# Small products of the triangular inverse, issued round the tiles of the array instead of tile by tile

## The chip, the cores and the metric

One core of a Trainium2 chip runs the whole model in one launch. The metric is the device time of an execution in microseconds; the figure for a kernel is the median of its runs.

## What is computed

Two layers of a diffusion block over 512 latent and 256 context tokens of width 1024. Each layer projects its normalised input once, runs three mixers in parallel on parts of the projection (neighbourhood attention, a bidirectional gated DeltaNet with four heads, a Fourier mixer), merges them by gates, and ends in an MLP. The change lies in the DeltaNet, whose recurrence is solved chunk by chunk:

```python
def _gated_delta_chunked(q, k, v, g, beta, s0):
    '''S_t = a_t (I - b_t k_t k_t^T) S_{t-1} + b_t k_t v_t^T, o_t = S_t^T q_t (chunked WY form)'''
    ...
    a_mat = jnp.where(strict, jnp.einsum('bhncd,bhnsd->bhncs', kb, k) * decay, 0.0) + jnp.eye(c, dtype=jnp.float32)
    rhs = jnp.concatenate([v * beta[..., None], kb * jnp.exp(g)[..., None]], axis=-1)
    sol = lax.linalg.triangular_solve(a_mat, rhs, left_side=True, lower=True)
    ...
    s_fin, o = lax.scan(step, s0, xs)
```

For each chunk a triangular matrix with ones on its diagonal must be solved against. The kernel inverts it instead and lets the scan multiply by the inverse.

## The kernel before

The kernel works in chunks of 128 tokens: six chunks and two directions make twelve blocks of 128x128 a head (`NU` is 12). `layer(l)` runs once a layer; in it, `by_clock` merges four generators by the times that they claim: `stream_dn` (the scan), `stream_prep` (what the scan needs, one `dn_prep(h)` for each of the four heads), `stream_na` (attention) and `stream_in` (input projections). This gives each instruction a priority, and a scheduler then orders the instructions of every engine by priority and by when their inputs can be ready. So the order on an engine isn't written out anywhere, and DMAs issued by SP form one queue of their own, in which a DMA that waits for its buffer holds back all behind it. A projection product (line 245, `ps_in`, `ps_inc`) is fed by `wload` (line 230): a weight load `wr` on SP, then a split into two parts on ScalarE and on VectorE or GpSimd.

`dn_prep(h)` does this: it loads the decay rows of its head twice, `Df` and `Db` (lines 531 and 532, SP); VectorE makes three decay masks of them (lines 538 to 540, `Dl` in a third buffer); products `ps_kk` give the triangular matrices `N` and the score matrices `PT`. The four 32x32 blocks on each diagonal go through DRAM (`nd`) to a layout with one block on a partition, VectorE inverts them, and they come back through `wd` into `N` and, transposed, into `Tst` (lines 592 and 593, eight DMAs on SP). Then the inverse is put together in two steps, the lines that the change touches:

- *32 to 64.* `ps_r` (line 601): for each of two quadrants `q`, twelve 32x32 products, at array position (32, 0) for the first and (96, 64) for the second; ScalarE copies each quadrant to `R` (603). `ps_w`: for each quadrant the products of line 609 at (0, 32) or (64, 96) and those of 613 at (0, 0) or (64, 64); 12 and 6 products for the first quadrant, 6 and 12 for the second; behind each quadrant ScalarE writes the results, negated, to `N` (616) and `Tst` (617).
- *64 to 128.* `ps_r2` (625): two groups of six 64x64 products at (64, 0), copied to `R` (627). `ps_w2` (630) at (0, 0) and `ps_w3` (636) at (0, 64), six products each, each in a PSUM tile of its own, copied out at 632 and 638. `L` is then copied from `Tst` (641, ScalarE) and `N` (642, VectorE); `dn_step` begins with products on it (`ps_ch`).

An array position (row, column) names the part of TensorE's 128x128 array that a product lies on: the row is that of its input partitions, the column that of its output partitions in PSUM. All PSUM tiles named here come from one tag with a single buffer (`pp`), so each waits for the one before to be read. `Df`, `Db`, `Dl`, the two blocks of the diagonal inverse and `R` share a tag of three SBUF buffers (`pr`), so the next head's loads wait for buffers of this head's inverse. All products here are float32.

Of the kernel before, what the change touches and what calls it, by code (L numbers as in the profile page):

```python
# [17 lines left out]
P = 128  # L18
# [19 lines left out]
# gates computed beside the mixers  # L38
NPRE = 16
# columns of the vector block  # L40
# [4 lines left out]
def kernel(ctx: ExitStack, tc: tile.TileContext, A: dict, out: bass.AP):  # L45
# [75 lines left out]
    def sigmoid_into(dst, src):  # L121
        """exp(min(x, 0) - log(1 + exp(-|x|))); dst is not src"""
        act.activation(out=dst, in_=src, func=AF.Abs)
        act.activation(out=dst, in_=dst, func=AF.Exp, scale=-1.0)
        act.activation(out=dst, in_=dst, func=AF.Ln, bias=1.0)
        dve.scalar_tensor_tensor(dst, in0=src, scalar=0.0, in1=dst, op0=ALU.min, op1=ALU.subtract)
        act.activation(out=dst, in_=dst, func=AF.Exp)

# [9 lines left out]
    def ada_block(l, q):  # L138
        """columns 512*q .. 512*q+511 of the adaLN projection of layer l, the contraction in four column groups"""
# [16 lines left out]
    def ada_group(l, q, lag):  # L156
        """four such blocks from the one at q, one in each column group; loads run lag rows of tiles ahead"""
# [26 lines left out]
    def ada_scale(l, i, k0=0, n=KD):  # L184
        """norm weight * (1 + scale) of the norm i of layer l"""
        sc = MOD[l][:, (3 * i + 1) * 8 + k0:(3 * i + 1) * 8 + k0 + n, :]
        g = vecs[l][:, (V_N1, V_N2)[i] + k0:(V_N1, V_N2)[i] + k0 + n]
        o = SC[l][i][:, k0:k0 + n, :]
        dve.tensor_scalar(o, sc, 1.0, None, op0=ALU.add)
        dve.tensor_tensor(o, o, g.unsqueeze(2).to_broadcast([P, n, 2]), op=ALU.mult)  # L190
# [22 lines left out]
    def ada_upto(l, q):  # L213
        """what follows needs the block q of layer l"""
# [8 lines left out]
    wcnt = [0]  # L223

    def wload(src, kn=KD):
        """[P, kn, 128] float32 -> for each k two float32r parts whose sum is the float32 one"""
# [13 lines left out]
    def proj(ps, w, kn, xh, xl, segs, off=0, k0=0, k1=KD):  # L240
        """ps[:, seg - off] = sum_k w[:, k].T @ x[k][:, seg], of it the part from k0 to k1"""
# [6 lines left out]
    def split_act(src, w, name, alloc):  # L248
        """float32 SBUF tile -> (hi, lo) tiles"""
# [7 lines left out]
    class Rms:  # L257
        """1 / rms of each token; the last of the tiles goes straight to the sum over partitions"""
# [33 lines left out]
    def mod_norm(l, i, xs, w, nm):  # L292
        """the modulated norm as two parts"""
# [24 lines left out]
    def modulate(k, x):  # L318
        """the first modulation, of a normalised tile that is no longer needed"""
# [10 lines left out]
    def by_clock(pri, *streams):  # L330
        """merge generators that yield the time of what they have emitted, by their clocks"""
# [33 lines left out]
    def layer(l):  # L365
# [39 lines left out]
        def gates():  # L405
# [40 lines left out]
            # rows of the summed log-decays, for a broadcast over partitions  # L446
# [7 lines left out]
        odn = drp.tile([NDH, P, TT], F32, tag="odn", bufs=1, name="odn")  # L454

        def conv_silu(ps, cw, w):
            """short conv over tokens and silu; the result at [0:512] and [514:770]"""
# [41 lines left out]
        def tok_major(src, offs, name, tag):  # L499
            """[feature, token] -> [token, 6, feature]"""  # L500
# [23 lines left out]
        def dn_prep(h, st):  # L524
# [41 lines left out]
            # inverses of the 32x32 diagonal blocks, one block on each partition  # L566
# [28 lines left out]
            # merge 32 -> 64  # L595
            R = U("R", tag="pr", w=NU * 64).rearrange("p (u c) -> p u c", c=64)
            ps = ps_aux("ps_r", "pp")
            for q in range(2):
                a, b = slice(64 * q, 64 * q + 32), slice(64 * q + 32, 64 * q + 64)
                for u in range(NU):  # L600
                    pe.matmul(ps[a, u * 32:u * 32 + 32], lhsT=Nu[b, u, a], rhs=Tst[b, u, b], start=True, stop=True,
                              tile_position=(64 * q + 32, 64 * q))
                act.copy(R[a, :, 0:32], ps[a, 0:NU * 32].rearrange("p (u c) -> p u c", c=32))
            ps = ps_aux("ps_w", "pp")
            for q in range(2):
                a, b = slice(64 * q, 64 * q + 32), slice(64 * q + 32, 64 * q + 64)
                ul = slice(0, NU) if q == 0 else slice(6, NU)
                for u in range(ul.start, ul.stop):
                    pe.matmul(ps[b, u * 32:u * 32 + 32], lhsT=R[a, u, 0:32], rhs=Nu[a, u, a], start=True, stop=True,
                              tile_position=(64 * q, 64 * q + 32))  # L610
                ut = slice(0, 6) if q == 0 else slice(0, NU)
                for u in range(ut.start, ut.stop):
                    pe.matmul(ps[a, u * 32:u * 32 + 32], lhsT=Nu[a, u, a], rhs=R[a, u, 0:32], start=True, stop=True,
                              tile_position=(64 * q, 64 * q))
                pv = ps[:, 0:NU * 32].rearrange("p (u c) -> p u c", c=32)
# [3 lines left out]
            # merge 64 -> 128  # L619
# [9 lines left out]
            for u in range(6):  # L629
                pe.matmul(ps[a, u * 64:u * 64 + 64], lhsT=Nu[a, u, a], rhs=R[a, u, :], start=True, stop=True,  # L630
                          tile_position=(0, 0))
            act.activation(out=Tst[a, 0:6, b], in_=ps[a, 0:384].rearrange("p (u c) -> p u c", c=64), func=AF.Copy,
                           scale=-1.0)
            ps = ps_aux("ps_w3", "pp")
            for u in range(6):
                pe.matmul(ps[b, u * 64:u * 64 + 64], lhsT=R[a, 6 + u, :], rhs=Nu[a, 6 + u, a], start=True, stop=True,
                          tile_position=(0, 64))
# [8 lines left out]
        def dn_step(h, st, d, step):  # L646
            """one chunk of the scan of direction d"""
# [95 lines left out]
        ona = drp.tile([4, P, TT], F32, tag="ona", bufs=1, name="ona")  # L743

        def na_in(c, st):
            # scores as products of two parts each: the two halves of a stack hold the parts of one head
# [37 lines left out]
        def na_pair(scores, n_loc, biases, vts, dst, view):  # L784
            """softmax over the keys of 128 queries for both heads of a pair; the outputs to dst, feature-major"""
# [85 lines left out]
        ofn = drp.tile([4, P, TT], F32, tag="ofn", bufs=1, name="ofn")  # L871

        def fourier():
# [34 lines left out]
            for i, (s0, n, tab) in enumerate(sets):  # L908
# [24 lines left out]
                for g in range(4):  # L933
# [9 lines left out]
                    else:  # L943
                        # the transform at (n - t, -f) is the one at (t, f); -f lies 64 rows away, but for 0 and 64
# [167 lines left out]
        for hb in range(4):  # L1112
# [12 lines left out]
            for k in range(KD):  # L1125
# [3 lines left out]
                # the last one in halves of the tokens, so that the final norm starts early  # L1129
# [43 lines left out]
    # the first products with the first half of the features, while the rest of the modulation comes  # L1173
# [28 lines left out]
def _prepare(inp):  # L1202
# [31 lines left out]
    # relative bias of the two kinds of query tiles; outside the window a constant  # L1234
# [60 lines left out]
```

## Time and profile before

| | us |
|---|---|
| median of three runs | 2771.27 (2769.14 to 2774.12) |
| span of the profiled execution, first to last instruction | 2750.2 |
| TensorE busy in it | 2618.0 |
| VectorE busy | 1391.2 |
| ScalarE busy | 1191.1 |
| GpSimd busy | 609.1 |

The profile comes from one execution. It gives the span of that execution and no device time beside it, so the difference to the median, 21.1 us, stands for what lies before the first and behind the last instruction. An engine's busy time is the time in which at least one of its instructions ran. The chain that ended last is followed back from the last instruction, at each step to what released it; work on it is work that the end waited for. In the timeline, records of one kind that follow each other are put together, with their number behind an x; a record of TensorE lasts longer than the distance to the next, since products overlap in its pipeline.

### The profile page before, as it was taken

What the parts mean: (1) busy time and instruction counts of PE and PEld (TensorE: products, weight loads), DVE (VectorE), ACT (ScalarE), POOL (GpSimd) and SP (SyncE); (2) the same over time, 40 slices, a digit from 0 to 9 for tenths busy, and PEclk for the clock granted to TensorE, in tenths of its full rate; (3) what the DMA queues carried; (4) which work ended last, traced back from release to release, by engine and by line L of the source; (5) the groups of instructions that cost most, each with busy time, mean ns of one, the idle gap of its engine ahead of it and who ended that gap; (6) DMA issues with size and microseconds to landing.
All of it is one profiled execution on the core that took longest, in us unless ns stands there. A gap on an engine that the chain in (4) does not pass through costs nothing.

```text
span 2750.2 us, 40072 instructions
## 1 busy us (share of the span) xinstructions
PE 2618.0 (95%) x15066; PEld 2103.9 (77%) x15066; DVE 1391.2 (51%) x2831; ACT 1191.1 (43%) x2430; POOL 609.1 (22%) x522
## 2 busy tenths in 40 slices
PE   6999999999999999999999988998999999999998
PEld 3877768677878777888888867776777777788886
DVE  5657576857423634222222365768677436433334
ACT  4546555555543224121222255455565654423333
POOL 3222212231111112111111123221323222222222
PEclk9999999999999999999999999999999999999999
DMA  6232222221255743342312223232232335333332
GB/s 219 81 87 68 78 58 75 71 71 53 68 197 189 255 139 115 104 135 91 120 59 66 81 60 111 72 81 58 79 85 63 93 112 187 96 95 96 96 96 88
DMA packets 196705, 278.41 MB, mean 101 GB/s; under 512 B 56768, under 2 KB 75936, under 8 KB 196512
## 3 DMA queue, kind: packets, MB, share of 16 engines
q1 hardware_dynamic: 196512, 275.87, 32.9%
q8 instruction: 118, 1.93, 0.3%
q14 instruction: 75, 0.61, 0.1%
HBM read 244.29 MB, written 27.31 MB: 99 GB/s over the span
## 4 chain that ended last, share of the span: by engine, by line
PE 73%; DVE 8%; ACT 3%; DMA 1%; issue 1%; POOL 1%; SPq 0%; DVEq 0%; ACTq 0%; POOLq 0%
PE ps_m L245 32%; PE ps_in L245 14%; PE ps_br L245 6%; PE ps_wo L245 4%; PE ps_inc L245 3%; PE ps_ada L168 1%; DVE cy L468 1%; PE ps_s L830 1%; PE ps_s L818 1%; PE ps_s L829 1%; PE ps_s L812 1%; DVE xn L303 1%; PE ps_ch L676 1%; DVE stmp L581 1%; DMA Db<-gdr 1%
## 5 line engine op out<-in xcount | busy, mean ns | idle before, releaser
L236 POOL TENSOR_TENSOR wlo<-wr,whi 128x512 fp32r<-128x512 f32 x360 | 484.8, 1348 | 1894.7 <-ACT whi L233 1789.7
L233 ACT CAST whi<-wr 128x512 fp32r<-128x512 f32 x560 | 346.3, 619 | 879.9 <-PE ps_m L245 519.8
L245 PE MATMUL ps_in<-hh,whi 128*128 128x512 f32 x960 | 381.0, 408 | 11.8 <-ACT kraw L750 5.5
L245 PE MATMUL ps_in<-hh,wlo 128*128 128x512 f32 x960 | 378.2, 404 | 2.2 <-POOL wlo L236 2.2
L245 PE MATMUL ps_in<-hl,whi 128*128 128x512 f32 x960 | 377.7, 404 | 0.0
L236 DVE TENSOR_TENSOR wlo<-wr,whi 128x512 fp32r<-128x512 f32 x200 | 138.6, 693 | 244.7 <-ACT whi L233 243.9
L245 PE MATMUL ps_m<-ml,whi 128*128 128x512 f32 (+1 forms) x768 | 233.8, 358 | 4.1 <-POOL ml L313 3.2
L245 PE MATMUL ps_m<-mh,whi 128*128 128x512 f32 (+1 forms) x768 | 233.0, 358 | 2.9 <-ACT mh L309 2.9
L245 PE MATMUL ps_m<-ah,wlo 128*128 128x512 f32 (+1 forms) x776 | 234.4, 355 | 0.0
L245 PE MATMUL ps_m<-ah,whi 128*128 128x512 f32 (+1 forms) x776 | 234.2, 355 | 0.0
L245 PE MATMUL ps_m<-al,whi 128*128 128x512 f32 (+1 forms) x776 | 233.2, 353 | 0.0
L245 PE MATMUL ps_m<-mh,wlo 128*128 128x512 f32 (+1 forms) x768 | 231.7, 355 | 0.0
L245 PEld LDWEIGHTS ps_in<-hh,whi 128*128 128x128 f32 x960 | 181.8, 194 | 48.1 <-ACT kraw L750 5.9
L245 PEld LDWEIGHTS ps_in<-hh,wlo 128*128 128x128 f32 x960 | 181.2, 193 | 36.5 <-POOL wlo L236 3.4
L245 PEld LDWEIGHTS ps_in<-hl,whi 128*128 128x128 f32 x960 | 181.4, 194 | 32.8 <-issue 2.0
L1134 DVE SCALAR_TENSOR_TENSOR x<-ps_m,mod,x 128x512 f32<-128x512 f32 (+1 forms) x97 | 60.8, 655 | 247.8 <-PE ps_m L245 247.8
L245 PEld LDWEIGHTS ps_m<-mh,whi 128*128 128x128 f32 x768 | 126.6, 189 | 35.3 <-ACT whi L233 8.4
L245 PEld LDWEIGHTS ps_m<-ah,whi 128*128 128x128 f32 x776 | 127.7, 188 | 28.9 <-ACT whi L233 6.7
L245 PE MATMUL ps_inc<-hh,whi 128*128 128x256 f32 x512 | 149.6, 292 | 0.0
L245 PEld LDWEIGHTS ps_m<-ml,whi 128*128 128x128 f32 x768 | 126.8, 188 | 29.5 <-POOL ml L313 6.0
L245 PE MATMUL ps_inc<-hl,whi 128*128 128x256 f32 x512 | 148.7, 290 | 0.0
L245 PE MATMUL ps_inc<-hh,wlo 128*128 128x256 f32 x512 | 147.0, 287 | 0.0
(325 smaller groups left out, 4927.3 us busy)
## 6 DMA issues: line engine op xcount, KB each, us to landing
wr<-in_w_dram SPq DMA_DIRECT2D x256, 256.0 KB
wr<-in_wi_dram SPq DMA_DIRECT2D x224, 256.0 KB
wada<-in_wa_dram SPq DMA_DIRECT2D x192, 256.0 KB
wr<-in_wb_dram SPq DMA_DIRECT2D x48, 256.0 KB
wr<-in_wo_dram SPq DMA_DIRECT2D x32, 256.0 KB
gpre<-sgp SPq DMA_DIRECT2D x16, 384.0 KB
sgg<-gpre SPq DMA_DIRECT2D x16, 384.0 KB
rot<-kn SPq DMA_DIRECT2D x64, 64.0 KB
```

What stands on the lines that cost most here:

```text
L168: pe.matmul(ps[32 * j:32 * j + 32, :], lhsT=cs[:, k, :], rhs=ws[k][j], start=(k == 0), stop=(k == KD - 1), tile_position=(0, 32 * j))
L233: act.copy(hi, raw)
L236: eng.tensor_tensor(lo, raw, hi.bitcast(F32), op=ALU.subtract)
L245: pe.matmul(ps[:, s0 - off:s1 - off], lhsT=a, rhs=b[k][:, s0:s1], start=(k == 0 and i == 0), stop=(k == kn - 1 and i == 2))
L303: dve.scalar_tensor_tensor(t[:, s0:s1], in0=xs[k][:, s0:s1], scalar=sc, in1=rs[:, s0:s1], op0=ALU.mult, op1=ALU.mult)
L468: dve.scalar_tensor_tensor(y[:, :n], in0=cin[:, j:j + n], scalar=vec[:, cw + j:cw + j + 1], in1=y[:, :n], op0=ALU.mult, op1=ALU.add)
L581: dve.tensor_tensor(tv, Nb[:, j + 1:32, j:j + 1].to_broadcast([48, n, m]), Wb[:, j:j + 1, 0:m].to_broadcast([48, n, m]), op=ALU.mult)
L676: pe.matmul(ps[:, 2 * P:3 * P], lhsT=kt, rhs=Uc, start=True, stop=True)
L812: pe.transpose(ps[:, i * P:(i + 1) * P], Pm[:, i * P:(i + 1) * P], ident)
L818: pe.matmul(pss[0][f, 0:P], lhsT=v[:, f], rhs=Pt[:, i * P:(i + 1) * P], start=(i == 0), stop=(i == nk // P - 1), tile_position=(0, 64 * hh))
L829: pe.matmul(ps, lhsT=st["qd"][hh][:, q], rhs=st["ks"][hh][:, k], start=True, stop=False)
L1134: dve.scalar_tensor_tensor(x2[k][:, s0:s1], in0=ps[:, s0:s1], scalar=mod(l, 5, k, v), in1=x2[k][:, s0:s1], op0=ALU.mult, op1=ALU.add)
```

## The change

Loops over the twelve blocks become the outer loops, and the quadrants the inner ones, so that neighbouring products lie on different parts of the array. `ps_r`'s two copies to `R` come behind both quadrants' products, and `ps_w`'s four copies on ScalarE behind all 36 products. `ps_w3` loses its PSUM tile: its products alternate with those of `ps_w2` and write the other half of the partitions of the same tile. The comments are gone too. Lines behind 601 have moved by one to three.

```diff
+            quads = [(q, slice(64 * q, 64 * q + 32), slice(64 * q + 32, 64 * q + 64)) for q in range(2)]
-            for q in range(2):
-                a, b = slice(64 * q, 64 * q + 32), slice(64 * q + 32, 64 * q + 64)
-                for u in range(NU):
+            for u in range(NU):
+                for q, a, b in quads:
                     pe.matmul(ps[a, u * 32:u * 32 + 32], lhsT=Nu[b, u, a], rhs=Tst[b, u, b], start=True, stop=True,
                               tile_position=(64 * q + 32, 64 * q))
+            for q, a, b in quads:
                 act.copy(R[a, :, 0:32], ps[a, 0:NU * 32].rearrange("p (u c) -> p u c", c=32))
             ps = ps_aux("ps_w", "pp")
-            for q in range(2):
-                a, b = slice(64 * q, 64 * q + 32), slice(64 * q + 32, 64 * q + 64)
-                ul = slice(0, NU) if q == 0 else slice(6, NU)
-                for u in range(ul.start, ul.stop):
-                    pe.matmul(ps[b, u * 32:u * 32 + 32], lhsT=R[a, u, 0:32], rhs=Nu[a, u, a], start=True, stop=True,
-                              tile_position=(64 * q, 64 * q + 32))
-                ut = slice(0, 6) if q == 0 else slice(0, NU)
-                for u in range(ut.start, ut.stop):
-                    pe.matmul(ps[a, u * 32:u * 32 + 32], lhsT=Nu[a, u, a], rhs=R[a, u, 0:32], start=True, stop=True,
-                              tile_position=(64 * q, 64 * q))
+            uls, uts = (slice(0, NU), slice(6, NU)), (slice(0, 6), slice(0, NU))
+            for u in range(NU):
+                for q, a, b in quads:
+                    if uls[q].start <= u:
+                        pe.matmul(ps[b, u * 32:u * 32 + 32], lhsT=R[a, u, 0:32], rhs=Nu[a, u, a], start=True, stop=True,
+                                  tile_position=(64 * q, 64 * q + 32))
+                for q, a, b in quads:
+                    if u < uts[q].stop:
+                        pe.matmul(ps[a, u * 32:u * 32 + 32], lhsT=Nu[a, u, a], rhs=R[a, u, 0:32], start=True, stop=True,
+                                  tile_position=(64 * q, 64 * q))
+            for (q, a, b), ul, ut in zip(quads, uls, uts):
                 act.activation(out=Nu[b, ul, a], in_=pv[b, ul], func=AF.Copy, scale=-1.0)
                 act.activation(out=Tst[a, ut, b], in_=pv[a, ut], func=AF.Copy, scale=-1.0)
...
             ps = ps_aux("ps_w2", "pp")
             for u in range(6):
                 pe.matmul(ps[a, u * 64:u * 64 + 64], lhsT=Nu[a, u, a], rhs=R[a, u, :], start=True, stop=True,
                           tile_position=(0, 0))
-            act.activation(out=Tst[a, 0:6, b], in_=ps[a, 0:384].rearrange("p (u c) -> p u c", c=64), func=AF.Copy,
-                           scale=-1.0)
-            ps = ps_aux("ps_w3", "pp")
-            for u in range(6):
                 pe.matmul(ps[b, u * 64:u * 64 + 64], lhsT=R[a, 6 + u, :], rhs=Nu[a, 6 + u, a], start=True, stop=True,
                           tile_position=(0, 64))
+            act.activation(out=Tst[a, 0:6, b], in_=ps[a, 0:384].rearrange("p (u c) -> p u c", c=64), func=AF.Copy,
+                           scale=-1.0)
             act.activation(out=Nu[b, 6:NU, a], in_=ps[b, 0:384].rearrange("p (u c) -> p u c", c=64), func=AF.Copy,
                            scale=-1.0)
```

TensorE in the first head of layer 0, from the first products of `ps_w` to the next step of the merge, before (`x12` are twelve products in a row; `ps_sc` and `Pm` belong to attention):

```order
L609 MATMUL ps_w<-N,R 32x32 x12
L613 MATMUL ps_w<-R,N 32x32 x6
L829 MATMUL ps_sc<-ks,qd 128x256
L830 MATMUL ps_sc<-ks,qlo 128x256
L245 MATMUL ps_in<-hh,whi 128x512
L245 MATMUL ps_in<-hl,whi 128x512
L245 MATMUL ps_in<-hh,wlo 128x512
L609 MATMUL ps_w<-N,R 32x32 x6
L613 MATMUL ps_w<-R,N 32x32 x12
L245 MATMUL ps_in<-hh,whi 128x512
```

The same place now: the last products of `ps_w` and what follows up to `ps_r2`.

```order
L612 MATMUL ps_w<-N,R 32x32 x2
L616 MATMUL ps_w<-R,N 32x32
L612 MATMUL ps_w<-N,R 32x32 x2
L616 MATMUL ps_w<-R,N 32x32
L830 MATMUL ps_sc<-ks,qd 128x256
L831 MATMUL ps_sc<-ks,qlo 128x256
L245 MATMUL ps_in<-hh,wlo 128x512
L245 MATMUL ps_in<-hh,whi 128x512
L245 MATMUL ps_in<-hl,whi 128x512
L245 MATMUL ps_in<-hh,wlo 128x512
L813 MATMUL ps_sc<-ident,Pm 128x128 x2
L628 MATMUL ps_r_2105<-Tst,N 64x64 x6
```

Two blocks of `ps_w` with other work between them have become one of 36 products, three for each of the twelve `u`, and what stood between the blocks stands behind them. `ps_w2` and `ps_w3`, two blocks of six, have become one in the same way. `ps_r` has become one product by itself, some other work, and 23 products in a row:

```order
L602 MATMUL ps_r<-Tst,N 32x32
L813 MATMUL ps_s<-ident,Pm 128x128 x3
L819 MATMUL ps_s<-Pm,naV 64x128
L813 MATMUL ps_s<-ident,Pm 128x128 x4
L482 MATMUL ps_l_2337<-r_l_2335,ones 128x512
L245 MATMUL ps_in<-hh,whi 128x512
L819 MATMUL ps_s<-Pm,naV 64x128 x6
L482 MATMUL ps_l_2341<-r_l_2335,ones 128x256
L602 MATMUL ps_r<-Tst,N 32x32 x23
```

The second product, the first of the other quadrant, needs that quadrant's blocks from `wd`, which are the last to be loaded. This split is the same in all eight heads.

SP behind the first head's loads of the inverted blocks, before (`rot`, `kn` belong to the next head's rotary step, `bias` to attention, `gpre` to the gates):

```order
L593 DMA Tst<-wd 32x12x32
L531 DMA Df<-gdr 128x6x128
L532 DMA Db<-gdr 128x6x128
L230 DMA wr<-in_wi_dram 128x512
L493 DMA rot<-kn 32x512 x4
L230 DMA wr<-in_wi_dram 128x512
L835 DMA bias<-in_nab_dram 128x512 x2
L230 DMA wr<-in_wi_dram 128x512 x4
```

And now:

```order
L593 DMA Tst<-wd 32x12x32
L230 DMA wr<-in_wi_dram 128x512
L836 DMA bias<-in_nab_dram 128x512 x2
L230 DMA wr<-in_wi_dram 128x512
L493 DMA rot<-kn 32x512 x4
L531 DMA Df<-gdr 128x6x128
L532 DMA Db<-gdr 128x6x128
L230 DMA wr<-in_wi_dram 128x512 x4
```

The loads of `Df` and `Db` for the second head stood right behind the last `Tst`; now weight loads, the bias and the rot loads are ahead of them. In the next head, and in the first three of layer 1, they move back in the same way by two to eight loads; in the third head of layer 0 they stay where they were.

## Rows read from the trace of the kernel before

**Rows 1.** The page: span, busy time of each engine, and the chain by engine.

```profile
span 2750.2 us, 40072 instructions
...
PE 2618.0 (95%) x15066; PEld 2103.9 (77%) x15066; DVE 1391.2 (51%) x2831; ACT 1191.1 (43%) x2430; POOL 609.1 (22%) x522
...
PE 73%; DVE 8%; ACT 3%; DMA 1%; issue 1%; POOL 1%; SPq 0%; DVEq 0%; ACTq 0%; POOLq 0%
```

**Rows 2.** Windows of the mixers' nine stretches, their sum: us, busy of each engine.

```profile
sum 1057.00, PE 993.83 PEld 788.27 DVE 699.90 ACT 592.60 POOL 260.25; mean PE 110.43 PEld 87.59 DVE 77.77 ACT 65.84 POOL 28.92
```

**Rows 3.** Groups by line: records | busy us, mean ns of one | idle before.

```profile
L630 PE MATMUL ps_w<-R,N 64*64 64x64 f32 x96 | 7.3, 222 | 0.0
```

**Rows 4.** Timeline of TensorE, first head: start us, us, engine line op xcount.

```profile
240.85 0.94 PE L601 MATMUL ps_r<-Tst,N 32*32 32x32 f32 x24
241.72 0.55 PE L812 MATMUL ps_s<-ident,Pm 128*128 128x128 f32 x3
...
247.56 0.39 PE L245 MATMUL ps_in<-hl,whi 128*128 128x512 f32 x1
247.79 0.39 PE L245 MATMUL ps_in<-hh,wlo 128*128 128x512 f32 x1
248.11 0.84 PE L609 MATMUL ps_w<-N,R 32*32 32x32 f32 x21
248.77 0.21 PE L613 MATMUL ps_w<-R,N 32*32 32x32 f32 x1
...
248.83 0.19 PE L613 MATMUL ps_w<-R,N 32*32 32x32 f32 x1
248.83 0.19 PE L609 MATMUL ps_w<-N,R 32*32 32x32 f32 x1
...
249.26 0.39 PE L829 MATMUL ps_sc<-ks,qd 128*128 128x256 f32 x1
249.58 0.38 PE L830 MATMUL ps_sc<-ks,qlo 64*128 64x256 f32 x1
...
256.59 0.91 PE L630 MATMUL ps_w<-R,N 64*64 64x64 f32 x12
257.43 0.65 PE L818 MATMUL ps_sc<-Pm,naV 128*64 128x128 f32 x6
```

**Rows 5.** The same view near 785 us, a product on four column tiles.

```profile
785.28 1.06 PE L168 MATMUL ps_ada<-wada,cs 128*32 128x512 f32 x8
```

**Rows 6.** The chain of waits, 2159 to 2182 us, by line.

```profile
by line: PE ps_in L245 65.9%; PE ps_r L601 7.6%; PE ps_r L625 7.3%; PE ps_w L609 5.2%; PE ps_w L613 4.8%; PE ps_w L630 3.6%; PE ps_w L636 3.6%; PE ps_ch L672 1.9%; PE ps_ch L676 1.2%
```

**Rows 7.** Timeline of ScalarE, the copies behind the first block of ps_w.

```profile
249.37 0.48 ACT L616 ACTIVATE N<-ps_w 32x384 f32<-32x384 f32 x1 [0.63 <-PE ps_w L613]
249.86 0.32 ACT L617 ACTIVATE Tst<-ps_w 32x192 f32<-32x192 f32 x1
```

**Rows 8.** Timeline of SP's queue, first head.

```profile
235.26 0.54 SPq L532 DMA_DIRECT2D Db<-gdr  x1
...
250.67 0.91 SPq L835 DMA_DIRECT2D bias<-in_nab_dram  x2
```

**Rows 9.** The chain of waits, 395 to 445 us: start us, us, what.

```profile
407.05 0.87 PE ps_r L601 x24
...
414.07 10.31 DMA Db<-gdr
```

**Rows 10.** Timeline of VectorE, first and second head: [idle before <-releaser].

```profile
261.08 0.56 DVE L642 COPY L<-N 128x768 f32<-128x768 f32 x1
...
424.40 1.63 DVE L540 TENSOR_SCALAR Db<-Db,g_gc 128x128 f32<-128x128 f32 x6 [8.54 <-DMA Db<-gdr]
```

**Rows 11.** The chain of waits, 1686 to 1706 us, one load.

```profile
1688.60 6.79 DMA Df<-gdr
```

**Rows 12.** Timelines of SP and VectorE, first head of layer 1.

```profile
1811.56 0.86 SPq L835 DMA_DIRECT2D bias<-in_nab_dram  x2
...
1824.35 0.60 DVE L538 TENSOR_SCALAR Dl<-Df,g_gc 128x128 f32<-128x128 f32 x2 [1.43 <-ACT L L641]
```

More of the change, by code (lines that the diff above doesn't have):

```diff
@@ L597, in dn_prep @@
             ps = ps_aux("ps_r", "pp")
-            for q in range(2):
-                a, b = slice(64 * q, 64 * q + 32), slice(64 * q + 32, 64 * q + 64)
-                for u in range(NU):
+            quads = [(q, slice(64 * q, 64 * q + 32), slice(64 * q + 32, 64 * q + 64)) for q in range(2)]
+            for u in range(NU):
+                for q, a, b in quads:
                     pe.matmul(ps[a, u * 32:u * 32 + 32], lhsT=Nu[b, u, a], rhs=Tst[b, u, b], start=True, stop=True,
                               tile_position=(64 * q + 32, 64 * q))
+            for q, a, b in quads:
                 act.copy(R[a, :, 0:32], ps[a, 0:NU * 32].rearrange("p (u c) -> p u c", c=32))
             ps = ps_aux("ps_w", "pp")
-            for q in range(2):
-                a, b = slice(64 * q, 64 * q + 32), slice(64 * q + 32, 64 * q + 64)
-                ul = slice(0, NU) if q == 0 else slice(6, NU)
-                for u in range(ul.start, ul.stop):
-                    pe.matmul(ps[b, u * 32:u * 32 + 32], lhsT=R[a, u, 0:32], rhs=Nu[a, u, a], start=True, stop=True,
-                              tile_position=(64 * q, 64 * q + 32))
-                ut = slice(0, 6) if q == 0 else slice(0, NU)
-                for u in range(ut.start, ut.stop):
-                    pe.matmul(ps[a, u * 32:u * 32 + 32], lhsT=Nu[a, u, a], rhs=R[a, u, 0:32], start=True, stop=True,
-                              tile_position=(64 * q, 64 * q))
-                pv = ps[:, 0:NU * 32].rearrange("p (u c) -> p u c", c=32)
+            pv = ps[:, 0:NU * 32].rearrange("p (u c) -> p u c", c=32)
+            uls, uts = (slice(0, NU), slice(6, NU)), (slice(0, 6), slice(0, NU))
[9 more added lines that the diff above has]
+            for (q, a, b), ul, ut in zip(quads, uls, uts):
                 act.activation(out=Nu[b, ul, a], in_=pv[b, ul], func=AF.Copy, scale=-1.0)
@@ L631, in dn_prep @@
                           tile_position=(0, 0))
+                pe.matmul(ps[b, u * 64:u * 64 + 64], lhsT=R[a, 6 + u, :], rhs=Nu[a, 6 + u, a], start=True, stop=True,
+                          tile_position=(0, 64))
             act.activation(out=Tst[a, 0:6, b], in_=ps[a, 0:384].rearrange("p (u c) -> p u c", c=64), func=AF.Copy,
                            scale=-1.0)
-            ps = ps_aux("ps_w3", "pp")
-            for u in range(6):
-                pe.matmul(ps[b, u * 64:u * 64 + 64], lhsT=R[a, 6 + u, :], rhs=Nu[a, 6 + u, a], start=True, stop=True,
-                          tile_position=(0, 64))
             act.activation(out=Nu[b, 6:NU, a], in_=ps[b, 0:384].rearrange("p (u c) -> p u c", c=64), func=AF.Copy,
```

## The prediction, on record before the changed kernel ran

> **What bounds the kernel now.** I read the page's head first: TensorE is busy 95% of the 2750.2 us span and 73% of the chain that ended last [rows 1]. Then the stretches in which the mixers run, by windows, since only there do the changed lines work: TensorE is busy 993.8 of 1057 us, VectorE 700, ScalarE 593 [rows 2]. Then the chain inside one such stretch: of 23 us the projections hold 65.9% and the six lines of the merge 32.1% [rows 6]. So the merge is no side work there: TensorE goes from projections to a merge block and on to projections without idling, and a shorter block lets everything behind it start earlier.
>
> Not all of it lies so. In the second head of layer 0 the chain holds one merge block (407.05) and then goes through a transfer of 10.31 us, Db's load, and VectorE [rows 9]; VectorE had stood 8.54 us for that load [rows 10]. That is the second thing to follow: the loads of Df and Db.
>
> The 2750.2 us are first to last instruction of one execution; the median of three runs is 2771.27, so 21.1 us lie outside the span. Nothing of the change lies there, and I subtract from the median.
>
> **What a block costs, and why.** A product of the merge shows as two MATMUL records: twelve products of line 601 are x24 [rows 4]. Such a block of 24 records begins at 240.85 and the next work at 241.72, 0.87 us [rows 4]. Within a block, 21 records of line 609 begin between 248.11 and 248.77: 31.4 ns a step. 24 steps are 0.75, so 0.12 us is the drain behind the block. Ahead of it the projection product takes 0.32 us (247.79 to 248.11) where its neighbour takes 0.23 (247.56 to 247.79): 0.09 us. The block costs 0.87 + 0.09 = 0.96 us. A block of ps_w (36 records) runs from 248.11 to 249.26, 1.15, and costs 1.24; a 64x64 block of 12 records from 256.59 to 257.43, 0.84, and costs 0.93. Its records begin (0.91 - 0.22) / 11 = 62 ns apart [rows 3, 4], twice as far as at half the columns. So the step is the time in which a tile takes its columns, not a rate at which any instruction goes out.
>
> Per head two blocks of each kind: 2 x 0.96 + 2 x 1.24 + 2 x 0.93 = 6.26 us; eight heads, 50 us. The two 64x64 blocks of line 625 stay as they are.
>
> **Do tiles overlap?** Two places say so. Where line 609's tile gives way to line 613's, one record of either begins in the same hundredth of a microsecond, 248.83, and 613's first at 248.77 is ahead of that 609 although it comes later in the program: two tiles at work [rows 4]. And line 168's products on four column tiles, written alternating, take 1.06 us for 8 records of 512 columns, 0.13 us each, where a full-width product of 512 columns takes 0.23 [rows 5, 4]. Neither shows two tiles in different rows of the array, nor a whole block of small ones.
>
> [...]
>
> **The change, part by part.** The number of products and what each computes are as before.
>
> *ps_r.* The order puts one product alone, then other work, then 23 together. Alone: 2 x 0.031 + 0.21 = 0.27 us. The 23: 12 of one tile beside 11 of the other, if they overlap the length of 12: 0.96. So 1.92 becomes 1.24: -0.68.
>
> *ps_w.* All 36 stand in one block on four tiles of 12, 6, 6 and 12 products. With full overlap the longest decides, 0.96: 2.48 becomes 0.96, -1.52.
>
> *ps_w2 and ps_w3.* One block of 12 products on two column tiles, 0.93: 1.86 becomes 0.93, -0.93. One PSUM buffer of the single-buffered tag is taken once rather than twice; ScalarE reads both halves after the last product.
>
> Sum: -3.13 us a head, -25 us in all, with full overlap. The other end is no overlap: only the seams' 0.21 us go, once for ps_w and once for w2: -0.4 a head, -3 us. The nearest row for alternating tiles is line 168's, which overlaps throughout, and I take the full end.
>
> *Evacuation.* Before, ScalarE emptied the first half of ps_w while TensorE did the second. Now the four copies come behind the last product: 0.48 + 0.32 + 0.32 + 0.48 = 1.60 us [rows 7], and with the hand-over from TensorE (249.26 to 249.37) and back about 1.8, before the 64x64 products can start. TensorE's cover there, by the order: in the first head two ps_sc products of 0.32 (249.26 to 249.58), four projections of 0.23 [rows 4] and two transposes, some 1.9 us; over the eight heads 1.4 to 2.1. The missing pieces add up to about 0.5 us. Were there no cover, 8 x 1.8 = 14 us.
>
> *Loads of Df and Db.* The diff doesn't show this; the order does. These loads of the next head (lines 531, 532) were queued on SP right behind the inverse's blocks: Db at 235.26 in the first head. Now they stand behind weight loads, the bias and the rot loads; SP works in order, so they wait for what those wait for. The bias went out at 250.67 [rows 8], so Db goes out some 18 us later than it did, near 254. Such a load takes 6.79 to 10.31 us [rows 9, 11]: it lands at 261 to 264. Before, VectorE copied L at 261.08 among the work on Df [rows 10], and only then does the scan start. So in this head I count nothing of the gain. In the second the chain has only the first block before the load [rows 9]: 0.5. Third and fourth of layer 0: loads as before or none, 3.1 each. First head of layer 1: Db behind a bias that went out at 1811.56, landing 1819 to 1823, wanted at 1824.35 less the gain [rows 12]: half, 1.5. Second and third: behind two or three weight loads, about two thirds, 2 each. Fourth: 3.1. Sum 0 + 0.5 + 3.1 + 3.1 + 1.5 + 2 + 2 + 3.1 = 15.3; less 0.5, 14.8.
>
> **Forecast**: 2771.3 - 14.8 = 2756.5 us.
>
> **Rivals.**
>
> [...]
>
> *Nothing lost.* The loads land in time everywhere, and projections fill every hole: 2771.3 - 25 = 2746. For it: TensorE has hardly a gap in these stretches. Against: the moved loads.
>
> *The gain is spent waiting.* The scan's start is set by the loads or by VectorE, 66% busy in these stretches [rows 2], and TensorE meets the same waits earlier: the merge was on the chain because TensorE's queue is full, but something else is just as late. Then 2766 to 2771, no change.
>
> *Slower.* One mechanism: late Df and Db. In four heads (the first of layer 0, the first three of layer 1) the loads move back. If VectorE stands for each as long as it now stands in the second head, 8.54 us [rows 10], that is 34 us against a gain of 25: +9, 2780. It decides from 25 / 4 = 6.2 us of standing a head. Against it: VectorE's own wait is only on the path if the scan needs it next, and in layer 1 some 10 us lie between landing and use.
>
> **How the numbers follow.** Forecast 0.47, half the overlap 0.15, nothing lost 0.13, gain spent 0.17, slower 0.08. A measurement of this kernel tells about 0.2%, 5.5 us, from no change. The forecast, nothing lost and two thirds of the half-overlap case lie under 2765.7: faster 0.70. The rest of that case and the spent gain: same 0.22. Slower 0.08. The range reaches from nothing lost (2745, a little under it) to the median before (2771), which leaves out the slower case and the upper edge of the spent gain.
>
> **What would show it.** A block of ps_r's 23 products near 0.9 us in the timeline of the changed kernel, ps_w's 36 near 0.9 and w2's 12 near 0.85 would bear out the overlap; 1.5 and 1.5 the half of it; 2.2 none. Starts of records in the same hundredth of a microsecond on two tiles show it directly. TensorE waiting for ScalarE at the first 64x64 product by more than a few tenths would say the evacuation was under-priced. VectorE's waits at lines 538 to 540 for Df and Db show the loads: over 6 us in a head that had none makes the slower case. The forecast is wrong if TensorE's busy time falls by 25 us and the span does not.

## The result, and the profile after

The changed kernel took 2740.9 us in the median of its runs against 2770.9 for the kernel before, a ratio of 0.9885 with an interval of 0.9865 to 0.9906. The forecast was 2756.5 us, the range 2745 to 2771: the direction was right, the time lies 4 us under the range, and the gain of 30 us is twice the 14.8 that the sum gave. One of the four runs of the changed kernel took 4970 us, and one of a later kernel 12031 us; the ratio and all other figures below leave them out.

The two profiled executions don't show 30 us. The pages of the kernel after, span and busy time:

```profile
span 2734.5 us, 40056 instructions
...
PE 2594.7 (95%) x15066; PEld 2079.9 (76%) x15066; DVE 1389.1 (51%) x2831; ACT 1190.6 (44%) x2430; POOL 608.8 (22%) x522
```

Against [rows 1] the span is 15.7 us shorter: TensorE's busy time fell by 23.3, and its time without work, span less busy, rose from 132.2 to 139.8. So half of the measured 30 us is in the traces, close to the 14.8 of the sum, and the first question was where the rest is.

The blocks of the merge came out as worked out. The timeline of TensorE after the change, first head: start us, us, engine, line, records.

```profile
247.65 0.94 PE L602 MATMUL ps_r<-Tst,N 32*32 32x32 f32 x46
248.52 0.43 PE L819 MATMUL ps_s<-Pm,naV 128*64 128x128 f32 x2
...
250.62 0.21 PE L612 MATMUL ps_w<-N,R 32*32 32x32 f32 x1
250.63 0.22 PE L616 MATMUL ps_w<-R,N 32*32 32x32 f32 x2
250.67 0.19 PE L612 MATMUL ps_w<-N,R 32*32 32x32 f32 x1
250.68 0.20 PE L616 MATMUL ps_w<-R,N 32*32 32x32 f32 x2
...
251.50 0.39 PE L830 MATMUL ps_sc<-ks,qd 128*128 128x256 f32 x1
...
257.01 0.27 PE L633 MATMUL ps_w<-R,N 64*64 64x64 f32 x1
...
257.12 0.22 PE L633 MATMUL ps_w<-R,N 64*64 64x64 f32 x1
257.12 0.22 PE L635 MATMUL ps_w<-N,R 64*64 64x64 f32 x1
...
257.85 0.54 PE L819 MATMUL ps_sc<-Pm,naV 128*64 128x128 f32 x5
```

46 records of ps_r take 0.87 us, as 24 did in [rows 4]; 72 of ps_w take 0.88 us (250.62 to 251.50), where one block of 36 took 1.15; the 24 of ps_w2's block 0.84 (257.01 to 257.85), where 12 took 0.84. Records on different tiles begin in the same hundredth of a microsecond or the next (257.12 twice, 250.62 and 250.63). The tiles of ps_r differ in their rows as well and write one PSUM tile, so this overlap holds between row neighbours too.

### The profile page after: what moved, and what is told of

Read it like the earlier page. It is cut to its first block, busy times and chain, and to the rows that moved or that the text cites. A ratio compares the mean times of both kernels' runs of the same rounds, so it can differ in the third digit from the quotient of the medians.

```text
span 2734.5 us, 40056 instructions
## 1 busy us (share of the span) xinstructions
PE 2594.7 (95%) x15066; PEld 2079.9 (76%) x15066; DVE 1389.1 (51%) x2831; ACT 1190.6 (44%) x2430; POOL 608.8 (22%) x522
```

## The experiments

**The kernel before again.** Its runs lay near 2771, its profiled execution had a span of 2750. One of the two had to be explained.

> The kernel before, unchanged, for a second trace. The listed runs of the changed kernel lie 1.9 us above their spans, while the profiled execution of before had a span of 2750.2 us and its runs a median near 2771. Theory: the 1.9 us hold for before too, and its profiled execution was some 17 us faster than its usual ones; then this trace has a span near 2769, the blocks of the merge last the same 0.87, 1.15 and 0.84 us, and the 17 us stand in waits of one or two stretches. Rival: span 2750 again with 2771 beside it, about 20 us outside the span; then the change took away 14 us that no trace shows.

Measured: this profiled execution has a span of 2771.0 us, and its runs spread from 2753 to 2778. Run by run the time lies 1.7 to 2.2 us above the span, for both kernels. So the 21.1 us were not outside the span; the first profiled execution of before was about 18 us faster than its usual ones. The overview by core, span and mean granted clock, first of the first trace of before, then of this one:

```profile
core 0: 2750.2 us, clock 0.981
```

```profile
core 0: 2771.0 us, clock 0.973
```

And the page of this one:

```profile
PE 2638.7 (95%) x15066; PEld 2119.8 (76%) x15066; DVE 1389.7 (50%) x2831; ACT 1191.8 (43%) x2430; POOL 607.1 (22%) x522
```

The same 15066 records kept TensorE busy for 2638.7 us instead of the 2618.0 of [rows 1], and its time without work was 132.3 us against 132.2. So the 20.8 us lie in products that took longer, and not in waits, as the theory had it: the granted clock is the difference. Windows show where: their length, the busy time of each engine, and behind these the granted clock. This trace around the first head's merge:

```profile
248.00:258.00 10.00, 9.43 (x126) 6.88 (x125) 4.87 (x10) 7.69 (x19) 2.75 (x5) 0.99 0.39 103
258.00:278.50 20.50, 20.50 (x120) 15.03 (x120) 10.34 (x25) 8.11 (x17) 1.70 (x2) 0.50 0.13 39
278.50:300.00 21.50, 21.28 (x147) 18.80 (x146) 14.38 (x44) 11.78 (x33) 8.13 (x8) 1.00 0.09 25
```

And the first trace of before at the same place:

```profile
240.00:250.00 10.00, 9.42 (x127) 6.87 (x127) 4.87 (x10) 7.68 (x18) 2.56 (x5) 1.00 0.36 102
250.00:270.00 20.00, 20.00 (x181) 16.46 (x181) 15.95 (x41) 13.81 (x35) 3.91 (x7) 1.00 0.14 41
```

For 20.5 us the granted clock is 0.50, the lower of the two values that the first trace of before shows (0.50 in 20 stretches of 3.4 to 10.2 us, 106.8 us in all, and 1.00 in the rest), and 120 records of TensorE go through where 181 went in 20 us. Before the fall TensorE worked on the same products in both (126 and 127 records in 10 us), 84 of them of the merge, with 0.6 us of waiting. In one execution the clock then fell, in the other not. In the 10 us ahead of each of the first trace's 20 falls TensorE stood for 0.4 to 3.3 us.

So for every run its time at the lower clock can be estimated from its mean, as if its clock too had only these two values: 2 x (1 - clock) x span. Over the 90 runs of before whose clock is on record, from 0.970 to 0.983, the span rises by 0.39 us for each us at the lower clock, with a correlation of 0.96. The table has the kernels of the whole study; its last column is the mean span less 0.39 us for each us at the lower clock, which compares them at equal clock; its standard error is 0.2 us for the kernel before, 0.4 for the changed one and 0.6 to 1.4 for the others. That of the time at the lower clock is 2 us for the kernel before, 3 for the changed one and 2 to 7 for the others.

| kernel | runs | median us | mean clock | us at lower clock | span at equal clock |
|---|---|---|---|---|---|
| before | 90 | 2766.9 | 0.9759 | 133 | 2711.7 |
| changed | 15 | 2745.8 | 0.9779 | 121 | 2696.8 |
| only ps_w2 and ps_w3 | 12 | 2751.7 | 0.9787 | 117 | 2706.2 |
| only ps_r and ps_w | 10 | 2747.6 | 0.9776 | 123 | 2698.1 |
| changed, quadrants swapped | 12 | 2740.9 | 0.9792 | 114 | 2694.0 |
| before, ps_r and ps_w doubled | 6 | 2830.1 | 0.9607 | 223 | 2742.4 |
| changed, ps_r and ps_w doubled | 11 | 2776.5 | 0.9723 | 154 | 2715.4 |
| changed, all four doubled | 6 | 2793.1 | 0.9707 | 164 | 2729.4 |
| changed, loads on ScalarE's queue | 12 | 2772.2 | 0.9734 | 147 | 2712.7 |
| changed, loads on GpSimd's queue | 12 | 2763.3 | 0.9747 | 139 | 2707.2 |

**The changed kernel again**, twice, for the question whether its few runs were lucky.

> The changed kernel again, for more runs and a second trace. Over 39 runs of before, the span follows the mean granted clock (correlation 0.96): 2750 us at 0.983, 2776 at 0.970. Theory: the gain has two terms, the shorter blocks at equal clock, 12 to 16 us, and fewer stretches at the lower clock, some 11 to 15 us of the median; then these runs lie near 2741 with a mean clock of 0.979 to 0.983, none below 0.976. Rival: the three runs of the changed kernel were lucky in the clock as its profiled run of before was; then they spread like before's, 0.970 to 0.983, 2735 to 2762, and the median lies near 2754.

> The changed kernel beside the two others. Its runs had a median of 2741 on one occasion and 2748 on another. Theory that the granted clock makes the difference: at equal clock its span lies 12 to 15 us under that of before on this chip too; mean clock 0.977 to 0.981, 2740 to 2749.

Measured: 2748.5 us, ratio 0.9936 (0.9916 to 0.9955), clocks 0.976 to 0.978; and 2745.1 us, ratio 0.9931 (0.9906 to 0.9957), clocks 0.974 to 0.980. The first theory was right in its two terms and wrong in the clocks, of which none reached 0.979; its rival was right that the first runs were lucky. The second expectation was met. The two terms are 2711.7 - 2696.8 = 14.9 us at equal clock, and 12 us less at the lower clock, which at 0.39 are 5 us. The first three runs lay 5 us under the pooled 2745.8, as the first runs of before were 4 us above its pooled 2766.9. Runs of equal clock say it without a fit: at 0.978 six runs of before took 2759.1 to 2761.2 us and five of the changed kernel 2743.4 to 2747.2.

**Half the change each.** The edits: only the last step's products alternate, or only those of the first.

```diff
             ps = ps_aux("ps_w2", "pp")
             for u in range(6):
                 pe.matmul(ps[a, u * 64:u * 64 + 64], ..., tile_position=(0, 0))
+                pe.matmul(ps[b, u * 64:u * 64 + 64], ..., tile_position=(0, 64))
...
```

> Only ps_w2 and ps_w3 alternate in one PSUM tile; ps_r and ps_w stay as in the kernel before. The SP order of layer 0 is that of before; in layer 1 only the loads of Df and Db for the third and fourth head move, by two and five places. Theory that TensorE's time is what counts: 8 x 0.93 = 7.4 us less, 2763 to 2764. Rival, that what counts is the moved order of the loads and what it does to the waits: the order is mostly that of before, so under 3 us, 2768 to 2771.

```diff
-            for q in range(2):
-                for u in range(NU):
+            for u in range(NU):
+                for q, a, b in quads:
                     pe.matmul(ps[a, u * 32:u * 32 + 32], ..., tile_position=(64 * q + 32, 64 * q))
...
```

> Only ps_r and ps_w go round the tiles; ps_w2 and ps_w3 stay as in the kernel before. The SP order is that of the changed kernel in layer 0 and in the first half of layer 1. Theory that TensorE's time counts: 8 x (0.68 + 1.52) = 17.6 us less, 2753. Rival, that the moved loads and their waits count: nearly all of the 30 us, 2741 to 2745.

Measured: 2751.7 and 2747.6 us. These figures are under what TensorE's time gives from a base of 2771, but the clock is in them: at equal clock they gain 5.5 of 7.4 us and 13.6 of 17.6. The first keeps the loads of layer 0 where they were and gains three quarters of its products' time; the second moves them and gains as large a share. So neither rival came: the moved loads are not what makes the gain, and nothing shows that they eat much of it here. The two together would be 19.1 us; the whole change has 14.9, and why 4 us are lost together isn't shown. The time at the lower clock doesn't follow the products: the first half, which takes 7.4 us of them away, has 117 us of it and the second, with 17.6, has 123, where the whole change has 121.

**The first product of ps_r with the others.** The quadrant loaded last goes first:

```diff
             for u in range(NU):
-                for q, a, b in quads:
+                for q, a, b in quads[::-1]:
                     pe.matmul(ps[a, u * 32:u * 32 + 32], ...
```

> The changed kernel with the quadrants of ps_r in the other order, so that the first product is one of the quadrant whose blocks are loaded last, and all 24 wait for them together. The single product with its switch of 0.27 us a head, and its drain, goes: TensorE's time falls by 8 x 0.25 = 2 us, 2739. Rival: the first product alone costs nothing, since TensorE had no other work then, or the block of 24 now begins later: 2741 or up to 2 us more.

> The changed kernel with ps_r's quadrants in the other order, again, beside the changed kernel on the same chip. Theory: 8 x 0.25 us of TensorE's time less, 2 us faster than the changed kernel. Rival: no difference over 1 us.

Measured: 2740.6 us, and on another occasion 2740.9 beside 2745.1 for the changed kernel; 2.8 us less at equal clock, against 2 expected. The ratios to before on that occasion, 0.9905 (0.9877 to 0.9933) and 0.9931 (0.9906 to 0.9957), have intervals that overlap, so a gain over the changed kernel is likely and not proven. It is the fastest of all that ran.

**Do stretches of small products bring the lower clock?** Each product of ps_r and ps_w is issued twice, tile by tile in the kernel before, round the tiles in the changed one; the second writes the same result over the first.

```diff
                 for u in range(NU):
                     pe.matmul(ps[a, u * 32:u * 32 + 32], lhsT=Nu[b, u, a], ...
+                    pe.matmul(ps[a, u * 32:u * 32 + 32], lhsT=Nu[b, u, a], ...
...
```

> The kernel before with every product of ps_r and ps_w issued twice, tile by tile. TensorE's time rises by 8 x (2 x 0.75 + 2 x 1.08) = 29 us. Theory that stretches of such products bring the lower clock: the stretch at the lower clock that one trace of before shows from the first head's ps_w on (20 us long) comes in nearly every run and in more heads; mean clock 0.965 to 0.970, 2768 + 29 + 10 to 20 = 2807 to 2817. Rival, that the clock's falls come from TensorE's waits, which these products don't change: clock 0.975, 2797.

> The changed kernel with every product of ps_r, ps_w, ps_w2 and ps_w3 issued twice, still round the tiles, the second writing the same result over the first. TensorE's time rises by 8 x (0.75 + 0.76 + 0.70) = 17.7 us, so its merge lasts nearly as long as before's. Theory that the clock falls after long stretches of small products whatever their order: the mean clock falls towards 0.976 and the median lies at 2741 + 18 + 7 = 2766. Rival, that it falls where products use one tile after another: the clock stays near 0.980, 2758. If the added products are hidden in waits: 2741 to 2750.

Measured tile by tile: 2830.1 us, above the theory's 2807 to 2817, at a mean clock of 0.957 to 0.965. Its windows around the merges of the first, third and fourth head:

```profile
240.00:250.00 10.00, 10.00 (x159) 7.79 (x158) 4.30 (x10) 7.59 (x18) 2.78 (x5) 1.00 0.36 100
250.00:274.00 24.00, 24.00 (x206) 18.70 (x203) 11.06 (x26) 7.91 (x18) 1.67 (x1) 0.51 0.12 37
...
575.00:585.00 10.00, 10.00 (x220) 8.97 (x219) 6.75 (x15) 4.95 (x13) 1.44 (x4) 1.00 0.15 45
585.00:602.00 17.00, 17.00 (x83) 13.94 (x84) 4.50 (x14) 8.57 (x16) 3.08 (x2) 0.50 0.16 53
715.00:725.00 10.00, 10.00 (x139) 7.72 (x138) 4.25 (x17) 3.69 (x14) 0.00 (x0) 1.00 0.01 2
725.00:752.00 27.00, 27.00 (x241) 23.40 (x241) 6.14 (x21) 9.09 (x32) 0.00 (x0) 0.50 0.04 16
```

TensorE doesn't wait at all in the 10 us before these falls, and works through them; five heads have one of 17 us or more. The rival, that falls come only from waits, is out for them. The added 29 us of products brought 90 us at the lower clock. Whether 29 us of other work, of full-width products for instance, would do the same wasn't tried.

Measured with all four doubled round the tiles: 2793.1 us, far above both expectations. This run decided nothing on the order: TensorE stood for 8.0 us once and 5.0 us once in or beside the doubled blocks for no cause that the profile shows, and 9.5 us for ScalarE, which the other doubled kernel hadn't. So only ps_r and ps_w were doubled round the tiles:

> The changed kernel with every product of ps_r and ps_w issued twice, round the tiles: the counterpart of the run in which the same products of before were doubled tile by tile, and where the granted clock fell five times for 17 to 27 us while TensorE was busy without a gap. TensorE's time rises by 8 x (0.75 + 0.76) = 12 us. Theory that products on one tile after another bring the falls: none over 14 us, none that begins while TensorE hasn't waited, time at the lower clock within 15 us of the changed kernel's 121, median 2746 + 12 = 2758 to 2763. Rival, that long stretches of small products bring them whatever the order: per us of added products as in the other run, 89 us for 29, so 37 us more at the lower clock and falls of 17 us or more in several heads, 2746 + 12 + 14 = 2772.

Measured: 2776.5 us, 154 us at the lower clock, 33 more than the changed kernel: near the rival's 37, not the theory's 15. Of the long falls that the rival wanted in several heads there is one, of 20.5 us, in the trace. Its windows around the longest of its falls:

```profile
2060.00:2070.00 10.00, 9.24 (x240) 7.91 (x239) 5.38 (x7) 4.97 (x10) 0.60 (x1) 1.00 0.72 200
2071.00:2091.50 20.50, 16.82 (x116) 12.88 (x116) 6.79 (x19) 9.83 (x18) 3.08 (x2) 0.51 0.15 46
```

And what TensorE waited for from 2060 to 2076 us: sum, count, longest.

```profile
PE ps_w L615 <- issue: 5.4, 1, 5.4
```

The theory that the order brings the falls is not borne out. Per us of added products both orders brought about as much time at the lower clock (33 for 12 us, 90 for 29). But here TensorE stood ahead of or at the start of four falls of 10 us or more in the mixers: for 1.0 to 3.8 us in the 10 us ahead of three of 10.2 us, and for 5.4 us at this one, for which the profile names no releaser, while tile by tile the long falls begin in work without a gap. So with small products doubled the time at the lower clock was longer in either order (223 us against 133, 154 against 121); in the tile-by-tile order the long falls come without a wait, in the other products and waits can't be told apart in these runs.

**When the loads go out.** The loads of Df and Db on ScalarE's queue, and on GpSimd's, out of SP's order:

```diff
-            sp.dma_start(out=Df, ...
-            sp.dma_start(out=Db, ...
+            act.dma_start(out=Df, ...
+            act.dma_start(out=Db, ...
```

> The changed kernel with the loads of Df and Db issued on ScalarE's queue, so that SP's order cannot hold them back. Theory that the moved loads still cost something: the changed trace shows VectorE waiting 16 us in all for lines 538 to 540, of which 9.4 us in heads 2 of layer 0 and 1 and 2 of layer 1; if half of it is on the path, 4 us faster, 2736 to 2737. Rival: those waits lie beside other work, 2741; or ScalarE, which then issues the loads behind its own work, brings them later, 2742 to 2748.

> The changed kernel with the loads of Df and Db issued on GpSimd's queue, between its weight splits. On ScalarE's queue they made the kernel 24 us slower. Theory that it is when the loads land that counts: if GpSimd gets to them before SP did, VectorE's waits for lines 538 to 540 (36 us in the changed trace, 20 of them for the first load of each layer) fall by 8 to 10 us and the time by 3 to 5 us; if it gets to them later, waits and time rise together. Rival, that the kernel got slower since ScalarE itself was held up by its queue: here GpSimd is 22% busy, and the time stays within 3 us of the changed kernel.

Measured: 2772.2 and 2763.3 us, 16 and 10 us slower than the changed kernel at equal clock. ScalarE's queue is slower than even the rival of later loads had it (2742 to 2748 us). On GpSimd's the second branch of the theory came, later loads and more time, and the rival's 3 us are out. The time at the lower clock was 147 and 139 us against 121, though no product was added. VectorE's waits with the loads on ScalarE's queue: sum, count, longest.

```profile
DVE Dl L538 <- DMA Df<-gdr: 24.5, 3, 9.6
DVE Db L540 <- DMA Db<-gdr: 21.1, 5, 10.8
...
DVE Db L540 <- DMA rot<-kn: 7.1, 1, 7.1
```

In the changed kernel they were 20.0 us, 6.4, and 7.3 where another DMA came last:

```profile
DVE Dl L538 <- DMA Df<-gdr: 20.0, 2, 11.5
...
DVE Db L540 <- DMA wr<-in_wi_dram: 7.3, 2, 5.3
DVE Db L540 <- DMA Db<-gdr: 6.4, 3, 4.4
```

What it leads to stands in VectorE's timeline with ScalarE's queue, first head of layer 1:

```profile
1833.80 2.65 DVE L540 TENSOR_SCALAR Db<-Db,g_gc 128x128 f32<-128x128 f32 x6 [2.18 <-DMA Db<-gdr]
...
1839.23 0.55 DVE L643 COPY L<-N 128x768 f32<-128x768 f32 x1
```

ScalarE wrote the last part of N at 1834.24, and L is copied from it 5 us later, behind the masks that had waited for Db. This is the slower rival's mechanism at work: over the whole trace TensorE's scan waits 15.0 us for that copy, against 3.7 in the changed kernel. Not all of it is the loads: VectorE also waits 14.4 us for ScalarE before that copy.

On GpSimd's queue TensorE waits 9.1 us for ScalarE's copy to `R` before ps_w2, against 2.2. These are two waits, in the first two heads of layer 1, and both lead back to the mask on Db, which waited for its load. VectorE, then ScalarE and TensorE in the first of them:

```profile
1827.83 1.62 DVE L540 TENSOR_SCALAR Db<-Db,g_gc 128x128 f32<-128x128 f32 x6 [6.44 <-DMA Db<-gdr]
...
1829.49 0.84 ACT L543 ACTIVATE Db<-Db 128x768 f32<-128x768 f32 x1 [4.11 <-DVE Db L540]
1830.24 0.46 ACT L630 COPY R<-ps_r 64x384 f32<-64x384 f32 x1
...
1830.75 0.27 PE L633 MATMUL ps_w<-R,N 64*64 64x64 f32 x1 [3.30 <-ACT R L630]
```

The exponential of Db's mask (line 543, at 1829.49) stands ahead of the copy (1830.24) on ScalarE, and waits 4.11 us for the mask, which waits 6.44 us for the load. GpSimd issued this load at 1818.31, behind a wait of 13.8 us for ScalarE at its weight splits; on SP it went out at 1802.98. So on either queue late loads cost time by a path that the traces show; but another queue rearranged more than the loads, and how much each part costs stays open.

## Why the prediction was right and wrong

*The base, wrong.* This is the first step that failed: "The median of three runs is 2771.27, so 21.1 us lie outside the span. Nothing of the change lies there, and I subtract from the median." Outside the span lie 1.7 to 2.2 us. The other 19 were inside the spans of the other runs: in the second trace of before the 20.8 us more are busy time of TensorE at the lower clock. The profiled execution (clock 0.981) was one of before's fastest, the three listed runs, whose clock isn't on record, of the slower ones by their times. The base for a comparison of many runs is 2766.9, and forecasting from that would have given 2752, against 2745.8 pooled. The pooled median lies inside the stated range, at its low end; the first runs lay under it by the luck of the draw.

*The clock, left out.* This is the second step that failed: the sum has no term for the granted clock, which puts it at nothing without a reason. The changed kernel spends 12 us less at the lower clock (121 against 133), some 5 us of the gain. That its shorter stretches of small products are the cause is not shown: doubling them raised that time, but the half changes, with 7.4 and 17.6 us less of them, lowered it by 16 and 10 us. The 30 us are thus about 15 of shorter blocks, 5 of the clock, and 9 of which runs were compared (4 above the pooled median of before, 5 under that of the changed kernel). The low end of the range, the full 25 us from the median, had left out that a gain in TensorE's time could come with one in its clock. The 2746 of the case that nothing is lost is next to the pooled 2745.8 by chance: the base was 4 us too high, and of the 25 us only 14.9 came.

*The overlap, right in each size.* 0.87, 0.88 and 0.84 us for the blocks that were to take 0.87, 0.87 and 0.84 without their entry. No run shows the half of the overlap, which has 0.15 of the chances and was to be seen by 1.5 us for each of the first two blocks: ps_r's 46 records on two tiles in different rows, which write one PSUM tile, took 0.87 us, and ps_w's 72 on four tiles that write one took 0.88, their starts 10.7 ns apart in the mean.

*The realised share, right in sum.* 14.8 was forecast, 14.9 is measured at equal clock. TensorE's time without work shows most of what was lost of the 25 us: 138.0 to 141.6 us in three traces of the changed kernel, 132.2 and 132.3 in the two of before, 6 to 9 us more. The parts came out otherwise than in the sum:

- Evacuation, 0.5 us in the sum, is 1.7 to 2.7 in the trace. The groups of lines after the change, with the time that TensorE stood before them, and line 625 of before, which is 628 now (ps_w2, line 630 then, had no such time either, [rows 3]):

```profile
L625 PE MATMUL ps_r<-Tst,N 64*64 64x64 f32 x192 | 14.5, 222 | 0.0
...
L628 PE MATMUL ps_r<-Tst,N 64*64 64x64 f32 x192 | 14.9, 223 | 2.7 <-ACT Tst L620 1.7 <-issue 0.9
...
L633 PE MATMUL ps_w<-R,N 64*64 64x64 f32 x96 | 7.9, 233 | 2.2 <-ACT R L630 2.2
```

  The copies themselves took what [rows 7] said, 0.48 and 0.32 us. Of the 1.7 us, 0.86 are in the first head of layer 1, where ScalarE began them 1.4 us after the last product, behind other work:

```profile
1804.56 1.68 ACT L756 CAST ks<-kraw 64x768 fp32r<-64x768 f32 x2
1806.26 0.48 ACT L619 ACTIVATE N<-ps_w 32x384 f32<-32x384 f32 x1
```

  The step took the cover from TensorE's order and left out ScalarE's. For the 0.9 us of line 628 the profile names no releaser. The 2.2 us of line 633 are no evacuation of ps_w, but the load of Db, in the same head.

- Loads. In the first head Db went out at 252.50, near the 254 of the sum, and L was copied at 261.47 (261.08 in [rows 10]); but ps_r began 1.4 us later than in [rows 4], so from there to the copy 1 us was gained where the sum counted none. TensorE, SP's queue and VectorE's timeline:

```profile
242.22 0.24 PE L602 MATMUL ps_r<-Tst,N 32*32 32x32 f32 x2
...
252.50 0.57 SPq L532 DMA_DIRECT2D Db<-gdr  x1
...
261.47 0.55 DVE L643 COPY L<-N 128x768 f32<-128x768 f32 x1
```

  In the second head the order on SP changed and the time did not: Db went out at 414.37, before at 414.07 ([rows 9]), behind other DMAs either way. VectorE's wait for it fell from the 8.54 us of [rows 10] to 1.99, since other work now stands ahead of the masks; the first mask came 0.7 us earlier (424.40 in [rows 10]), the copy of L 1.2, where 0.5 us was allowed. That copy before, and the lines of now:

```profile
427.23 0.56 DVE L642 COPY L<-N 128x768 f32<-128x768 f32 x1
```

```profile
414.37 1.03 SPq L532 DMA_DIRECT2D Db<-gdr  x1
...
418.69 3.00 DVE L468 SCALAR_TENSOR_TENSOR cy<-cin,vecs,cy 128x770 f32<-128x770 f32 x2
423.68 0.35 DVE L540 TENSOR_SCALAR Db<-Db,g_gc 128x128 f32<-128x128 f32 x1 [1.99 <-DMA wr<-in_wi_dram]
...
426.06 0.55 DVE L643 COPY L<-N 128x768 f32<-128x768 f32 x1
```

  In the first head of layer 1 the load cost the 2.2 us by the path that was seen with GpSimd's queue: mask, exponential, copy to `R`. Here the profile puts the mask's wait down to a weight load, but line 540 reads no DMA's data other than Db:

```profile
1812.63 1.63 DVE L540 TENSOR_SCALAR Db<-Db,g_gc 128x128 f32<-128x128 f32 x6 [5.31 <-DMA wr<-in_wi_dram]
...
1814.30 0.84 ACT L543 ACTIVATE Db<-Db 128x768 f32<-128x768 f32 x1 [2.98 <-DVE Db L540]
1815.05 0.46 ACT L630 COPY R<-ps_r 64x384 f32<-64x384 f32 x1
...
1815.56 0.32 PE L633 MATMUL ps_w<-R,N 64*64 64x64 f32 x1 [2.17 <-ACT R L630]
```

  So the loads cost less than the sum had in the two heads where it took off most, and cost elsewhere by a path through ScalarE that it didn't have; the copies cost more. That the sum still came to 14.8 is luck: the errors cancelled.

*The slower case* did not come, though its mechanism exists: with the loads on ScalarE's queue the whole gain at equal clock was gone (2712.7 against 2711.7), in part by it. Its point of decision, 6.2 us of VectorE standing a head, was not reached: apart from the first loads of a layer, where VectorE stood 10.9 us before and 11.5 after, 5.3 us was the most.

## What to carry to other kernels

Before subtracting from a median, see whether the profiled execution is one of the runs: where its span and the median differ by more than the constant that lies outside (1.7 to 2.2 us here), part of the difference is inside other executions, and the mean granted clock of the runs tells how much (here 0.39 us of span for each us at the lower clock). Compare two kernels at equal granted clock, and treat what a change does to the clock as a term of its own. Small products that lie on separate tiles can alternate between them, as here (72 records on four tiles in 0.88 us); what then decides is what stands ahead of the copies behind the block, in the copying engine's order as well as in TensorE's: here it was a cast (0.86 us of TensorE standing), or an instruction that waited for a load (2.2 us).

## What was not expected of the hardware

TensorE can be busy without a gap and be granted 0.50 all the same: with the 32x32 products of ps_r and ps_w doubled tile by tile, 24.00 of 24.00 us busy at 0.51 behind 10.00 of 10.00 us at 1.00, in the first head's merge. Whether this happens varies from execution to execution of one kernel: the same products were followed by 20.5 us at 0.50 in one trace of before and by 20 us at 1.00 in the other. Four tiles that differ in rows and columns and write one PSUM tile took 72 records in 0.88 us, a mean of 10.7 ns from start to start within the block (0.76 us over 71 steps).
